# A SwiGLU first pass: every second tile summed as three 256-column products, and its head cut into pairs of channel tiles

## The chip, the core and the metric

The kernel runs on one core of a Trainium2 chip. The metric is the device time of one execution in microseconds (us). A core has a matrix engine (TensorE, "PE" in the profile; its weight loads are listed apart as "PEld"), VectorE ("DVE"), ScalarE ("ACT"), GpSimd ("POOL", unused here), and a sync engine ("SP") whose queue issues all DMA transfers of this kernel. Each engine works through its own list of instructions in the order in which the program was built.

## The reference

One layer of an encoder block on 256 tokens of 2048 channels, all in 32-bit floats: a half-step SwiGLU feed-forward, attention in two groups of heads, and a second half-step SwiGLU feed-forward. Each of the three is preceded by a norm that is shifted and scaled by vectors computed from a conditioning vector `c`, and followed by a gate of the same origin:

```python
mod = jax.nn.silu(c) @ w_ada[l] + b_ada[l]
sh1, sc1, gt1, sh2, sc2, gt2, sh3, sc3, gt3 = jnp.split(mod, N_MOD, axis=-1)
f = swiglu(modulate(rms_norm(h, g_ffn1[l]), sh1, sc1), w1_gate[l], w1_up[l], w1_down[l])
h = h + 0.5 * gt1[:, None, :] * f
# swiglu(x) = (silu(x @ w_gate) * (x @ w_up)) @ w_down ; modulate(n) = n * (1 + scale) + shift
```

The inner width is 5632. The weights (half a gigabyte with `w_ada`) are read once each.

## The kernel before

**Layout and arithmetic.** Activations are kept transposed: channels on the 128 partitions, the 256 tokens in the free dimension. So there are 16 channel tiles k and 44 inner tiles f. The matrix engine multiplies in a reduced form of 32-bit float ("fp32r"). To keep the precision each operand is split in a high part, rounded to that form, and a low part, the rest. Of the four products three count: high x high, high x low, low x high. `nx[k]` holds both parts of channel tile k of the modulated norm side by side (256 high and 256 low columns). `mm2` (L171) forms the three products with two matmuls: the weight's high part against all 512 columns (L173), and its low part against the 256 high columns (L174). The product with the activation's low part thus lands in a second half of the PSUM tile and has to be added to the first half later. `mm3` (L176, matmul on L179) does it with three matmuls of 256 columns that all sum into one half; attention uses it.

**The weights' way.** Weights come as a stream of chunks of 128 x 1024 floats, 8 blocks of 128 x 128, in the order of use. For each chunk one DMA fills one of five raw buffers (`wraw`, L157), ScalarE casts the high part "hiw" (L167) and VectorE subtracts it for the low part "low" (L168); there are four buffers of each part. `W.chunk` (L327) keeps the stream three chunks ahead of the matmuls.

**The modulation** (`w_ada`, 18432 columns of 2048) runs in the background. A step loads 128 columns of 2048 numbers (1 MB, tiles "ra" and "rx", L138, three buffers in all) and VectorE multiplies and sums them against a broadcast of silu(c) (L147). Two of them, shift and scale, let one channel tile of the norm be formed (`norm_mod`, L241: L244 on VectorE, L247 on ScalarE, L248 on VectorE; L155 prepares the scale). How many such steps go with a chunk is set by `ws.pace(rate)`: each chunk fetched adds `rate` to a credit, and each whole credit is one step. `bg_until(n)` forces steps until no more than n are left.

**The first feed-forward.** It starts while the norm isn't complete. The first 8 inner tiles take channel tiles 0 to 5 as these come (L494, plain 32-bit matmuls). Then comes the first part, the loop at L506: inner tiles 8 to 31 take channel tiles 0 to 5 (`up_first`, L355). For each tile (gate and up columns, 12 blocks, one and a half chunks) `mm2` sums into a PSUM tile "pa", ScalarE copies the first half to a tile "pt" (L359), and VectorE adds the second half (L360). In the meantime the other ten channel tiles become ready at the rate `RA`. Then `ffn` (L407) begins. Its head takes the first four inner tiles ("pb", four PSUM tiles, all there are) through the remaining channel tiles in two cuts, 6 to 11 and then 12 to 15, each cut for all four tiles; after the second a tile is finished by `up_finish` (L371: two additions of PSUM halves, tanh, products and a split). The remaining 28 of the first 32 tiles then take channel tiles 6 to 15 one after the other, the down projection of these 32 follows ("pd"), then 12 more tiles and their down projection. The second feed-forward has the same form, with 8 channel tiles in its first part and cuts at 8, 12 and 16.

**What sets the order.** The program is built as a list of instructions with dependencies, and a planner with a cost model of its own orders each engine's instructions by readiness and priority, the place in the program being the priority unless `high_priority` raises it. Here that order is planned; only attention's matmuls are placed by hand. A VectorE instruction that waits holds up everything behind it.

Of the kernel before, what the change touches and what calls it, by code (L numbers as in the profile page):

```python
# [16 lines left out]
S = 256  # L17
D = 2048
KT = D // P
# [6 lines left out]
CW = 1024  # L26
K1 = 6
K2 = 8
KM = 12
NF0 = 8  # L30
NF1 = 4
NL = 4
ND = 3
F1 = 32
# [1 line left out]
PLAN_L = ((4, 6, 9, 11), (6, 8, 11, 13), (7, 9, 12, 14), (9, 11, 14, 15))  # L36
QS = 1
PACT = 0
RA = 0.475
RB = (0.28, 0.36, 0.36, 0.3)  # L40
RQ = 0.2
RE = 0.28
RF = (0.2, 0.2, 0.1, 0.1)
# [22 lines left out]
def build(tc, a):  # L66
    nc = tc.nc
    with ExitStack() as ctx:
# [5 lines left out]
        def psum_pool(kind):  # L74

            if "cm" in pools:
                pools.pop("cm").__exit__(None, None, None)
            if kind:
                pools["cm"] = tc.tile_pool(name=f"p{kind}", bufs=4 if kind == "pair" else 8,
                                           space=bass.MemoryType.PSUM, reuse_waits="tile")  # L80
                pools["p"] = pools["cm"].__enter__()

        def pair(nm):
            return pools["p"].tile([P, 2, 512], F32, tag="b", name=nm)
# [25 lines left out]
        nx = [cp.tile([P, 2, S], F32R, tag=f"nx{k}", name=f"nx{k}") for k in range(KT)]  # L110
# [9 lines left out]
        late = []  # L120
# [50 lines left out]
        def mm2(out, lh, ll, r, first, last):  # L171

            nc.tensor.matmul(out, lh, r, start=first, stop=False)  # L173
            nc.tensor.matmul(out[:, :S], ll, r[:, 0, :], start=False, stop=last)  # L174
# [6 lines left out]
        def split(src, hi, lo):  # L181
            nc.scalar.copy(hi, src)
            nc.vector.tensor_tensor(lo, src, hi.bitcast(F32), ALU.subtract)
# [168 lines left out]

        ws = W()

        def up_first(f, part, kx):  # L355
            ps = pair("pa")
            up_mm(ps, 0, kx, True, True)
            part[f] = hp.tile([P, 2, S], F32, tag="hid", name=f"pt{f}")
            nc.scalar.copy(part[f], ps[:, :, :S])  # L359
            nc.vector.tensor_tensor(part[f], part[f], ps[:, :, S:], ALU.add)  # L360
# [5 lines left out]
        def up_mm(ps, k0, k1, first, last):  # L366
            for j in range(2):
                for k in range(k0, k1):
                    mm2(ps[:, j, :], *ws.next(), nx[k], first and k == k0, last and k == k1 - 1)

        def up_finish(f, ps, part, hid):  # L371
            if f in part:
                t = part[f]
                nc.vector.tensor_tensor(t, t, ps[:, :, :S], ALU.add)
            else:
                t = hp.tile([P, 2, S], F32, tag="hid", name="gu")
                nc.scalar.copy(t, ps[:, :, :S])
            nc.vector.tensor_tensor(t, t, ps[:, :, S:], ALU.add)
            g_, u_ = t[:, 0, :], t[:, 1, :]
            th = sp.tile([P, S], F32, tag="nt", name="th")  # L380
            nc.scalar.activation(th, g_, AF.Tanh, scale=0.5)
            nc.vector.scalar_tensor_tensor(g_, th, 1.0, g_, ALU.add, ALU.mult)
            nc.vector.scalar_tensor_tensor(g_, g_, 0.25, u_, ALU.mult, ALU.mult)
            hid[f] = hp.tile([P, 2, S], F32R, tag="hid", name=f"hd{f}")
            split(g_, hid[f][:, 0, :], hid[f][:, 1, :])

        def ffn_down(fs, hid, gate, stat=None, out=None):
            acc_ = {}
            for d, f in down_order(fs):
                if d not in acc_:  # L390
                    acc_[d] = bank("pd")
                mm2(acc_[d], *ws.next(), hid[f], f == fs[0], f == fs[-1])
                if f != fs[-1]:
                    continue
                ps = acc_[d]
                g = gate(d)
                if d == KT - 1 and stat is not None:
                    idle(9)
                with tc.high_priority(offset=URGENT if stat is not None and d >= KT - 2 else 0):
                    for part_ in (ps[:, :S], ps[:, S:]):  # L400
                        nc.vector.scalar_tensor_tensor(h[d], part_, g, h[d], ALU.mult, ALU.add)  # L401
                    if stat is not None:
                        stat.add(h[d])
                if out is not None:
                    nc.sync.dma_start(out[d], h[d])

        def ffn(kx, part, ready_k, gate, rates, stat=None, out=None):  # L407


            hid = {}  # L410
            head = [pair("pb") for f in range(NF1)]
            ready_k(KM)
            for f in range(NF1):
                up_mm(head[f], kx, KM, True, False)
            ready_k(KT)
            late[:] = [True]
            ws.pace(rates[0])
            for f in range(NF1):
                up_mm(head[f], KM, KT, False, True)
                up_finish(f, head[f], part, hid)  # L420
            for f in range(NF1, F1):
                ps = pair("pb")
                up_mm(ps, kx, KT, True, True)
                up_finish(f, ps, part, hid)
            psum_pool("bank")
            ws.pace(rates[1])
            ffn_down(range(F1), hid, gate)
            psum_pool("pair")
            ws.pace(rates[2])
            for f in range(F1, FT):  # L430
                ps = pair("pb")
                up_mm(ps, 0, KT, True, True)
                up_finish(f, ps, {}, hid)
            ln_exp_set()
            psum_pool("bank")
            ws.pace(rates[3])
            ffn_down(range(F1, FT), hid, gate, stat, out)
# [5 lines left out]
        part = {}  # L443
# [41 lines left out]
        for k in range(K1):  # L485
# [4 lines left out]
            for j in range(2):  # L490
                w = ws.whole()
                for b in range(8):
                    f, q = 4 * j + b // 2, b % 2
# [10 lines left out]

        ws.pace(RA)
        for f in range(NF0, F1):  # L506
            up_first(f, part, K1)
        st = Stat(KT)

        def rest1(k):  # L510
# [6 lines left out]
        def once(l, fn):  # L517
            def get(d):
                if (l, d) not in gates:
                    gates[l, d] = fn(d)  # L520
                return gates[l, d]
            return get
# [3 lines left out]
        def gate1(d):  # L526
            bg_until(min(len(bg) + len(pend), 4 * KT - d - 1))
            return mods[2][:, d : d + 1]

        ffn(K1, part, rest1, once(1, gate1), RB, stat=st)  # L530
        ws.pace(0.0)
        bg_until(0)
        idle(14)
# [249 lines left out]
        part = {}  # L783
# [13 lines left out]
            bg_until(min(len(bg) + len(pend), KT - d - 1))  # L797
            return mods[8][:, d : d + 1]

        ffn(K2, part, rest2, once(3, gate3), RF, out=a["out"])  # L800
        psum_pool(None)
        ax_close()

# [38 lines left out]
def _arrays(inputs):  # L842
    g = {k: np.asarray(v) for k, v in inputs.items()}
    rope, lnc, nam, idx = _consts()
    c = np.ascontiguousarray

    def vec(v):
        return np.asarray(v).reshape(-1, P).T

    arr = {  # L850
        "x": c(g["x"][0].T.reshape(4, 4, P, S).transpose(0, 2, 1, 3)),
        "w_ada": c(g["w_ada"][0].reshape(D, 9 * KT, P).transpose(1, 2, 0)),
        "vecs": c(np.concatenate([
            vec(g["g_ffn1"][0]), vec(g["g_mix"][0]), vec(g["g_ffn2"][0]),
            vec(g["g_out_na"][0]), vec(g["g_out_dil"][0]), vec(g["c"][0]), vec(g["b_ada"][0])], axis=1)),
        "qkg": c(np.stack([g["qn_na"][0], g["kn_na"][0], g["qn_dil"][0], g["kn_dil"][0]])),
        "rope": rope, "lnc": lnc, "nam": nam,
        "nab": c(g["rpb_na"][0].reshape(8, -1)[:, idx].reshape(8, 2, P, S).transpose(0, 2, 1, 3)),
        "w_qkv": c(g["w_qkv"][0].reshape(8, 2, P, 3, 4, 512).transpose(4, 3, 0, 2, 1, 5)[:, ::-1].reshape(96, P, CW)),
        "w_o": c(g["w_o"][0].reshape(2, 8, P, KT, P).transpose(0, 3, 2, 1, 4).reshape(2 * KT, P, CW)),  # L860
    }

    def stream(blocks):
        return c(blocks.reshape(-1, 8, P, P).transpose(0, 2, 1, 3).reshape(-1, P, CW))

    for l in (1, 2):
        gu = np.stack([g[f"w{l}_gate"][0], g[f"w{l}_up"][0]]).reshape(2, KT, P, FT, P)
        gu = gu.transpose(3, 0, 1, 2, 4)
        kx = K1 if l == 1 else K2
        down = g[f"w{l}_down"][0].reshape(FT, P, KT, P).transpose(2, 0, 1, 3)  # L870

        def flat(x):
            return x.reshape(-1, P, P)

        arr[f"w{l}_a"] = stream(gu[NF0 if l == 1 else 0 : F1, :, :kx])
        arr[f"w{l}_b"] = stream(np.concatenate([
            flat(gu[:NF1, :, kx:KM]), flat(gu[:NF1, :, KM:]), flat(gu[NF1:F1, :, kx:])]))
        arr[f"w{l}_c"] = stream(gu[F1:])
        for nm, fs in (("d", range(F1)), ("e", range(F1, FT))):
            d, f = np.array(list(down_order(fs))).T  # L880
            arr[f"w{l}_{nm}"] = stream(down[d, f])
        if l == 1:
            arr["w1_s"] = stream(gu[:NF0, :, :K1].transpose(2, 0, 1, 3, 4))
    return arr
# [21 lines left out]
```

## Time and profile before

| | |
|---|---|
| median of 3 runs | 1902.46 us (1902.03 to 1902.89) |
| profiled execution, its own time | 1902.98 us |
| its span, first to last instruction | 1901.2 us |
| TensorE busy | 1873.3 us (99%) |
| weight loads busy | 1633.8 us (86%) |
| VectorE busy | 1563.3 us (82%) |
| ScalarE busy | 907.4 us (48%) |
| moved by DMA | 503.98 MB, mean 265 GB/s |
| mean granted TensorE clock | 0.996 |

How to read it: the rows of the profile have a start or a count and a busy time, the engine, the line of the kernel, the operation, and the tiles written and read. "[0.60 <-ACT pt L359]" means that the engine had been idle for 0.60 us and that ScalarE's instruction on L359, which wrote tile "pt", ended that. Matmuls are pipelined and their ends modelled, so the pace of the matrix engine is read from starts and counts, not from durations. The first part starts at about 63 us and the head at about 171 us of the span.

### The profile page before, as it was taken

What the parts mean: (1) busy time and instruction counts of PE and PEld (TensorE: products, weight loads), DVE (VectorE), ACT (ScalarE), POOL (GpSimd) and SP (SyncE); (2) the same over time, 40 slices, a digit from 0 to 9 for tenths busy, and PEclk for the clock granted to TensorE, in tenths of its full rate; (3) what the DMA queues carried; (4) which work ended last, traced back from release to release, by engine and by line L of the source; (5) the groups of instructions that cost most, each with busy time, mean ns of one, the idle gap of its engine ahead of it and who ended that gap; (6) DMA issues with size and microseconds to landing.
All of it is one profiled execution on the core that took longest, in us unless ns stands there. A gap on an engine that the chain in (4) does not pass through costs nothing.

```text
span 1901.2 us, 27533 instructions
## 1 busy us (share of the span) xinstructions
PE 1873.3 (99%) x10564; PEld 1633.8 (86%) x10564; DVE 1563.3 (82%) x2123; ACT 907.4 (48%) x1333; POOL 0.7 (0%) x6
## 2 busy tenths in 40 slices
PE   8999999999999999999999999999999999999999
PEld 6877888888888888888888888888888888888888
DVE  7899999988888889878887898888799986556565
ACT  2444545443334454555555565544555543334442
POOL 0000000000000000000000000000000000000000
PEclk9999999999999999999999999999999999999999
DMA  9988888889998987777765544888677876666664
GB/s 393 397 327 299 307 301 303 303 314 337 334 328 324 334 309 247 257 260 248 263 234 174 153 154 157 320 294 303 212 276 262 279 269 220 191 194 193 191 206 135
DMA packets 120227, 503.98 MB, mean 265 GB/s; under 512 B 13344, under 2 KB 15904, under 8 KB 101664
## 3 DMA queue, kind: packets, MB, share of 16 engines
q1 hardware_dynamic: 120096, 502.24, 75.9%
q8 instruction: 82, 1.34, 0.3%
q14 instruction: 49, 0.40, 0.1%
HBM read 500.09 MB, written 2.10 MB: 264 GB/s over the span
## 4 chain that ended last, share of the span: by engine, by line
PE 89%; DVE 6%; DMA 2%; ACT 1%; issue 1%; SPq 0%; ACTq 0%; DVEq 0%
PE pb L173 23%; PE pd L173 17%; PE pb L174 11%; PE pa L173 9%; PE pd L174 8%; PE pqk L179 5%; PE pqq L179 5%; PE pa L174 4%; PE pqv L179 4%; DVE low L168 2%; DMA rx<-in_w_ada_dram 2%; PE pso L173 1%; DVE rx L147 1%; DVE ra L147 1%; PE pso L174 1%
## 5 line engine op out<-in xcount | busy, mean ns | idle before, releaser
L167 ACT CAST hiw<-rw 128x1024 fp32r<-128x1024 f32 x644 | 674.6, 1050 | 713.1 <-PE pd L173 238.5
L168 DVE TENSOR_TENSOR low<-rw,hiw 128x1024 fp32r<-128x1024 f32 x644 | 785.9, 1222 | 264.3 <-ACT hiw L167 262.9
L173 PE MATMUL pb<-nx,hiw 128*128 128x512 f32 x1920 | 654.8, 389 | 0.0
L174 PE MATMUL pb<-nx,low 128*128 128x256 f32 x1920 | 530.8, 277 | 1.2 <-DVE low L168 1.2
L173 PE MATMUL pd<-hd,hiw 128*128 128x512 f32 x1408 | 480.1, 389 | 0.0
L173 PEld LDWEIGHTS pb<-nx,hiw 128*128 128x128 f32 x1920 | 360.3, 188 | 75.7
L174 PE MATMUL pd<-hd,low 128*128 128x256 f32 x1408 | 389.1, 276 | 0.0
L174 PEld LDWEIGHTS pb<-nx,low 128*128 128x128 f32 x1920 | 360.4, 188 | 1.9 <-DVE low L168 1.8
L173 PEld LDWEIGHTS pd<-hd,hiw 128*128 128x128 f32 x1408 | 264.3, 188 | 55.5
L173 PE MATMUL pa<-nx,hiw 128*128 128x512 f32 x800 | 275.1, 391 | 1.7 <-ACT hiw L167 1.2
L174 PEld LDWEIGHTS pd<-hd,low 128*128 128x128 f32 x1408 | 264.3, 188 | 0.0
L147 DVE CUSTOM_DVE_ANT_0 ra<-ra,cb,vec 128x2048 f32<-128x2048 f32 x101 | 237.0, 2346 | 3.3 <-DMA ra<-in_w_ada_dram 3.3
L174 PE MATMUL pa<-nx,low 128*128 128x256 f32 x800 | 220.9, 278 | 4.3 <-DVE low L168 4.3
L173 PEld LDWEIGHTS pa<-nx,hiw 128*128 128x128 f32 x800 | 149.5, 188 | 34.6 <-ACT hiw L167 2.4
L174 PEld LDWEIGHTS pa<-nx,low 128*128 128x128 f32 x800 | 150.2, 188 | 7.8 <-DVE low L168 6.8
L147 DVE CUSTOM_DVE_ANT_0 rx<-rx,cb,vec 128x2048 f32<-128x2048 f32 x43 | 100.9, 2347 | 1.5 <-DMA rx<-in_w_ada_dram 1.5
L173 PE MATMUL pso<-ox,hiw 128*128 128x512 f32 x256 | 90.4, 398 | 0.0
L179 PE MATMUL pqk<-hiw,nx 128*128 128x512 f32 x256 | 84.3, 395 | 0.0
L179 PE MATMUL pqq<-hiw,nx 128*128 128x512 f32 x256 | 83.0, 393 | 0.0
L179 PE MATMUL pqv<-hiw,nx 128*128 128x512 f32 x256 | 81.4, 392 | 0.3 <-ACT nx L247 0.3
L401 DVE SCALAR_TENSOR_TENSOR h<-pd,m,h 128x256 f32<-128x256 f32 x128 | 60.8, 482 | 20.0 <-PE pd L174 17.8
L174 PE MATMUL pso<-ox,low 128*128 128x256 f32 x256 | 71.6, 280 | 0.0
(138 smaller groups left out, 1510.0 us busy)
## 6 DMA issues: line engine op xcount, KB each, us to landing
ra<-in_w_ada_dram SPq DMA_DIRECT2D x101, 1024.0 KB, 7.2
rw<-in_w_b_dram SPq DMA_DIRECT2D x144, 512.0 KB, 4.5
rw<-in_w_d_dram SPq DMA_DIRECT2D x128, 512.0 KB, 4.2
rw<-in_w_a_dram SPq DMA_DIRECT2D x100, 512.0 KB, 5.2
rw<-in_w_c_dram SPq DMA_DIRECT2D x96, 512.0 KB, 4.1
rw<-in_w_qkv_dram SPq DMA_DIRECT2D x96, 512.0 KB, 4.1
rx<-in_w_ada_dram SPq DMA_DIRECT2D x43, 1024.0 KB, 7.3
rw<-in_w_e_dram SPq DMA_DIRECT2D x48, 512.0 KB, 4.5
```

Source lines behind the costliest of these rows:

```text
L147: ins = nc.vector.tensor_tensor_reduce(out=raw, in0=raw, in1=cb, scale=1.0, scalar=vec[:, BA + i : BA + i + 1], op0=ALU.mult, op1=ALU.add, ...
L167: casts[:] = casts[-1:] + [nc.scalar.copy(hi, raw)]
L168: lows[:] = lows[-1:] + [nc.vector.tensor_tensor(lo, raw, hi.bitcast(F32), ALU.subtract)]
L173: nc.tensor.matmul(out, lh, r, start=first, stop=False)
L174: nc.tensor.matmul(out[:, :S], ll, r[:, 0, :], start=False, stop=last)
L179: nc.tensor.matmul(out, l, r, start=first and i == 0, stop=last and i == 2, **kw)
L401: nc.vector.scalar_tensor_tensor(h[d], part_, g, h[d], ALU.mult, ALU.add)
```

## The change

Three things are edited, all in the first feed-forward's way of using channel tiles.

1. `up_first` gets a flag `slim`, set for even inner tiles (8, 10, ... 30: 12 of the 24 tiles of the first part). Such a tile uses `mm3` instead of `mm2`, so its three products sum into one half of PSUM, and is stored by `park`, one copy on ScalarE; the addition L360 does not exist for it.
2. The head of `ffn` takes a list of cuts. The first feed-forward's is 6, 8, 10, 12, 14, 16 instead of 6, 12, 16; the second's stays 8, 12, 16. The chunks of `w1_b` are laid out in the new order. The rate changes from `RA` to the next one ahead of the last cut, that is after 8 chunks of the head instead of 6.
3. `RA`, the modulation steps that go with one chunk of the first part, goes from 0.475 to 0.455.

```diff
-KM = 12
+CUTS = (6, 8, 10, 12, 14, 16)
+CUTS2 = (8, 12, 16)
...
-RA = 0.475
+RA = 0.455
...
-        def up_first(f, part, kx):
+        def up_first(f, part, kx, slim=False):
             ps = pair("pa")
+            if slim:
+                for j in range(2):
+                    for k in range(kx):
+                        wh, wl = ws.next()
+                        mm3(ps[:, j, :S], wh, wl, nx[k][:, 0, :], nx[k][:, 1, :], k == 0, k == kx - 1)
+                park(ps[:, :, :S], f, part)
+                return
             up_mm(ps, 0, kx, True, True)
...
-            ready_k(KM)
-            for f in range(NF1):
-                up_mm(head[f], kx, KM, True, False)
-            ready_k(KT)
-            late[:] = [True]
-            ws.pace(rates[0])
-            for f in range(NF1):
-                up_mm(head[f], KM, KT, False, True)
-                up_finish(f, head[f], part, hid)
+            for k0, k1 in zip(cuts, cuts[1:]):
+                ready_k(k1)
+                if k1 == KT:
+                    late[:] = [True]
+                    ws.pace(rates[0])
+                for f in range(NF1):
+                    up_mm(head[f], k0, k1, k0 == kx, k1 == KT)
+                    if k1 == KT:
+                        up_finish(f, head[f], part, hid)
...
-            up_first(f, part, K1)
+            up_first(f, part, K1, f % 2 == 0)
...
-        ffn(K1, part, rest1, once(1, gate1), RB, stat=st)
+        ffn(CUTS, part, rest1, once(1, gate1), RB, stat=st)
...
-        ffn(K2, part, rest2, once(3, gate3), RF, out=a["out"])
+        ffn(CUTS2, part, rest2, once(3, gate3), RF, out=a["out"])
...
-            flat(gu[:NF1, :, kx:KM]), flat(gu[:NF1, :, KM:]), flat(gu[NF1:F1, :, kx:])]))
+            *(flat(gu[:NF1, :, k0:k1]) for k0, k1 in zip(cuts, cuts[1:])), flat(gu[NF1:F1, :, kx:])]))
```

More of the change, by code (lines that the diff above doesn't have):

```diff
@@ L405, in ffn_down, with ffn @@
                     nc.sync.dma_start(out[d], h[d])
-        def ffn(kx, part, ready_k, gate, rates, stat=None, out=None):
+        def ffn(cuts, part, ready_k, gate, rates, stat=None, out=None):
+            kx = cuts[0]
             hid = {}
             head = [pair("pb") for f in range(NF1)]
-            ready_k(KM)
-            for f in range(NF1):
-                up_mm(head[f], kx, KM, True, False)
-            ready_k(KT)
-            late[:] = [True]
-            ws.pace(rates[0])
-            for f in range(NF1):
-                up_mm(head[f], KM, KT, False, True)
-                up_finish(f, head[f], part, hid)
+            for k0, k1 in zip(cuts, cuts[1:]):
[7 more added lines that the diff above has]
+                        up_finish(f, head[f], part, hid)
             for f in range(NF1, F1):
@@ L868, in _arrays @@
         gu = gu.transpose(3, 0, 1, 2, 4)
-        kx = K1 if l == 1 else K2
+        cuts = CUTS if l == 1 else CUTS2
+        kx = cuts[0]
         down = g[f"w{l}_down"][0].reshape(FT, P, KT, P).transpose(2, 0, 1, 3)
```

## The prediction

> **What bounds the kernel now.** I read the page first, then the busy time by stretches of 50 us, then waits, idle times and the order of instructions inside the one stretch where TensorE is not full.
>
> ```profile
> span 1901.2 us, 27533 instructions
> PE 1873.3 (99%) x10564; PEld 1633.8 (86%) x10564; DVE 1563.3 (82%) x2123; ACT 907.4 (48%) x1333; POOL 0.7 (0%) x6
> ```
>
> Busy time by stretches (columns: us, then PE, weight loads, VectorE, ScalarE, GpSimd busy with their counts, clock, DMA share, GB/s):
>
> ```profile
> 50.00:100.00 50.00, 47.87 (x257) 40.87 (x256) 43.95 (x49) 23.52 (x35) 0.00 (x0) 1.00 0.97 381
> ...
> 150.00:200.00 50.00, 47.06 (x269) 40.30 (x268) 45.57 (x55) 24.53 (x32) 0.00 (x0) 1.00 0.82 297
> 200.00:250.00 50.00, 50.00 (x296) 44.20 (x295) 49.78 (x69) 25.39 (x36) 0.00 (x0) 1.00 0.85 304
> 500.00:600.00 100.00, 100.00 (x589) 88.42 (x588) 81.73 (x86) 41.37 (x44) 0.00 (x0) 1.00 0.90 329
> ```
>
> TensorE is full from 200 us on, even where VectorE is busy for 49.78 of 50. Before that it is not, and the matmul counts (257 and 269 against 296) show more loss than the busy time does. The full pace is 100.00 us / 589 matmuls = 0.1698, so 0.340 us for one block (a 512-column matmul on L173 and a 256-column one on L174). The stretch is the first part (tiles "pa") and the head of four tiles behind it ("pb"); first starts, then groups between 62 and 210 us:
>
> ```profile
> L173 PE MATMUL pa<-nx,hiw x800: 387/389/503, 63.3 to 1351.6; 128*128 128x512 f32 x160
> L173 PE MATMUL pb<-nx,hiw x1920: 387/389/403, 171.3 to 1831.4; 128*128 128x512 f32 x192
> ...
> L174 PE MATMUL pa<-nx,low 128*128 128x256 f32 x288 | 80.0, 281 | 4.3 <-DVE low L168 4.3
> ```
>
> The 288 blocks take 171.3 - 63.3 = 108.0 us; at 0.340 they would take 97.8. **10.2 us are lost.** To what, the waits between 60 and 210 us say (total us, times, longest):
>
> ```profile
> ACT pt L359 <- PE pa L174: 52.9, 22, 3.6
> PEld pa L174 <- DVE low L168: 6.8, 9, 1.1
> ...
> DVE pt L360 <- ACT pt L359: 4.2, 9, 0.6
> PEld pa L173 <- ACT hiw L167: 2.4, 4, 0.8
> PEld pb L174 <- DVE low L168: 1.8, 2, 1.0
> SPq L159 <- DVE low L168: 107.3, 49, 4.8
> ```
>
> Weight loads wait 6.8 + 2.4 = 9.2 us in the first part (the remaining 1.0 is pace, below) and 1.8 in the head: **11.0 us of stall** in all. The DMA queue itself waits 107.3 us for VectorE to free raw buffers, so data aren't what is late. The order in one stall, VectorE and then TensorE:
>
> ```profile
> 79.06 2.34 DVE L147 CUSTOM_DVE_ANT_0 ra<-ra,cb,vec 128x2048 f32<-128x2048 f32 x1
> ...
> 81.33 0.68 DVE L360 TENSOR_TENSOR pt<-pt,pa 128x512 f32<-128x512 f32 x1
> 81.93 1.22 DVE L168 TENSOR_TENSOR low<-rw,hiw 128x1024 fp32r<-128x1024 f32 x1
> 83.06 0.48 DVE L248 SCALAR_TENSOR_TENSOR nx<-nt,m,nx 128x256 fp32r<-128x256 f32 x1
> 83.46 1.22 DVE L168 TENSOR_TENSOR low<-rw,hiw 128x1024 fp32r<-128x1024 f32 x1
> 85.28 0.69 DVE L360 TENSOR_TENSOR pt<-pt,pa 128x512 f32<-128x512 f32 x1 [0.60 <-ACT pt L359]
> 85.88 2.35 DVE L147 CUSTOM_DVE_ANT_0 rx<-rx,cb,vec 128x2048 f32<-128x2048 f32 x1
> ...
> 89.29 0.68 DVE L360 TENSOR_TENSOR pt<-pt,pa 128x512 f32<-128x512 f32 x1
> 89.89 0.15 DVE L155 SCALAR_TENSOR_TENSOR m<-m,vec 128x1 f32<-128x1 f32 x1
> ```
>
> ```profile
> 88.32 0.39 PE L173 MATMUL pa<-nx,hiw 128*128 128x512 f32 x1
> 89.43 0.39 PE L174 MATMUL pa<-nx,low 128*128 128x256 f32 x1 [0.72 <-DVE low L168]
> ```
>
> Chain: TensorE ends tile 12 (an even one), ScalarE copies it, VectorE, idle since 84.6, adds the other half (L360, 85.28), then the modulation product (85.88), and only then the low part that TensorE needs at 88.3; it starts again at 89.43, 1.1 instead of 0.23 us after its last matmul. From the addition to the end of the low part it is 89.29 - 85.28 = 4.0 us, plus some 0.6 for the copy: more than the 12 x 0.340 = 4.08 us that TensorE has for a tile.
>
> **The change part by part.**
>
> *One addition in two goes.* 12 of 24 tiles lose their L360. Starts one behind the other give what an instruction occupies: addition 81.93 - 81.33 = 0.60; low part 83.06 - 81.93 = 1.13; modulation product 81.33 - 79.06 = 2.27; the norm's steps 0.40 (83.46 - 83.06) twice and 0.15 (L155) for each two products, so 2.27 + 0.48 = 2.75 a product. Work of VectorE for two tiles (three chunks), before: 3 x 1.13 + 2 x 0.60 + 3 x 0.475 x 2.75 = 3.39 + 1.20 + 3.92 = 8.51 us, against 24 x 0.3396 = 8.15 of TensorE. VectorE bounds this stage, and its waits (4.2 for the copy) come on top: 9.0 measured (108.0 / 12). After: 3.39 + 0.60 + 3 x 0.455 x 2.75 = 7.74, which is 0.41 under TensorE; over 12 pairs 4.9 us of slack. ScalarE's copy stays as it is. So TensorE bounds, except where the order still puts a wait in front. The planner orders the engines anew, which I can't see. One such order costs more than VectorE's sum, the copy ahead of a cast:
>
> ```profile
> 93.63 0.59 ACT L359 COPY pt<-pa 128x512 f32<-128x512 f32 x1 [3.58 <-PE pa L174]
> 94.12 1.05 ACT L167 CAST hiw<-rw 128x1024 fp32r<-128x1024 f32 x1
> ...
> 95.22 0.50 PE L173 MATMUL pa<-nx,hiw 128*128 128x512 f32 x1 [0.26 <-ACT hiw L167]
> 96.48 0.39 PE L174 MATMUL pa<-nx,low 128*128 128x256 f32 x1 [0.76 <-DVE low L168]
> ```
>
> ScalarE idles 3.58 us until tile 14 (even) ends mid-chunk, and casts the next chunk only then; TensorE loses 0.26 + 0.76 idle and some 0.5 of refilling, 1.5 us (95.22 to 96.48 is 1.26 instead of 0.23 alone). The waits above hold four for a cast, 2.4 us in all, so some three of this size. The copy stays in the change, and 0 to 3 x 1.5 = 4.5 us may stay with it; I take one, 1.5, because the slack lets casts run ahead.
>
> *Three 256-column products instead of 512 + 256.* The columns are the same (768), with one matmul and one weight load more in each of 12 x 12 = 144 blocks. The kernel has such triples in attention; chain of waits, then matmuls by time, the first and the last of six:
>
> ```profile
> 870.39 0.70 PE po L179 x6
> ```
>
> ```profile
> 1118.16 0.28 PE L179 MATMUL po<-ph,vh 128*128 128x256 f32 x1
> ...
> 1118.73 0.28 PE L179 MATMUL po<-ph,vl 128*128 128x256 f32 x1
> ```
>
> That is 0.70 / 6 = 0.117 in the one place and 0.57 / 5 = 0.114 in the other: 0.342 to 0.351 for a triple against 0.340, so 144 x 0.002 to 0.011 = 0.3 to 1.6 us more. No run of triples longer than two is in this trace, so I let the cost go down to 0 and take 1.0. (The Trainium skill, page "TensorE: Matmul & The Clock Gate", section "Back-to-back issue gap", speaks against the change: in a stream of load-and-multiply pairs a 128-column matmul takes about 81 ns where an isolated one takes 56. If each matmul more cost those 25 ns, an estimate from that page is 144 x 0.025 = 3.6 us and a time near 1897; the rows above, with 114 to 117 ns for half of 227, show 1 to 4.) The same slower pace is in ordinary blocks too and explains the 1.0 us of the loss that isn't stall; I leave it as it is.
>
> *RA 0.475 to 0.455, and the head in five cuts.* 37 chunk loads fall to the pass and 6 to the head: 37 x 0.475 gives 17 modulation steps and 43 x 0.475 gives 20. Then 37 x 0.455 gives 16 and 45 x 0.455 gives 20. One product (2.75 us of VectorE) and its 1 MB transfer move from the pass to the head, past some chunk loads in SP's one queue, which has the time (it waits 107 us). The last channel tile is due after 64 blocks of the head rather than 48, 16 x 0.340 = 5.4 us later, which covers the 2.75; without that cover it would stand on TensorE's path in full. In the head the two waits (1.8 us) follow the last even tile and go with the rest. New is that the four head tiles end 4 x 0.340 = 1.36 us apart, not 2.72. Tile 4 needs the first one's PSUM, drained by two additions of L360's form (1.20), 4.1 us after that one ends; with a modulation product and a low part queued in front it takes 1.20 + 2.27 + 1.13 = 4.6, so 0 to 0.5 us; I take 0.3. The steps from there to the first down projection are the same (80 chunks less 6 or 8, and 74 x 0.28 and 72 x 0.28 both give 20), chunks are as many, and TensorE is full behind, so what is won here reaches the end.
>
> **Sum.** 11.0 - 1.5 (cast) - 1.0 (triples) - 0.3 (head) = 8.2 us. The profiled execution took 1902.98 (span 1901.2 and 1.8 around it), 0.5 above the median of 1902.46; from the median, 1902.5 - 8.2 = **1894.3 us**. With nothing left it is 11.0 + 0.5 of pace: 1891.0.
>
> **The rivals.**
>
> *The copy goes on holding back the cast* (0.17). Waits on ScalarE and triples at their worst: 11.0 - 4.5 - 1.6 - 0.5 = 4.4, 1898.1. For it: the copy is not removed and ScalarE idles 52.9 us for it. Against it: the waits above came where VectorE was behind.
>
> *DMA becomes the bound* (0.10). Sizes, and two stretches of 10 us:
>
> ```profile
> rw<-in_w_a_dram SPq DMA_DIRECT2D x100, 512.0 KB, 5.2
> ra<-in_w_ada_dram SPq DMA_DIRECT2D x101, 1024.0 KB, 7.2
> ```
>
> ```profile
> 70.00:80.00 10.00, 10.00 (x59) 8.79 (x58) 9.52 (x11) 3.73 (x5) 0.00 (x0) 1.00 1.00 403
> 130.00:140.00 10.00, 10.00 (x59) 8.75 (x58) 9.87 (x12) 4.50 (x6) 0.00 (x0) 1.00 0.98 358
> ```
>
> Two tiles at full pace need 3 x 0.524 + 1.365 x 1.049 = 3.00 MB in 8.15 us, 368 GB/s. If 358 is all there is, a pair takes 8.38, 12 x 0.23 = 2.8 us more: 1897.1. Against it stand 403 GB/s and the queue's idle time. (The Trainium skill, page "DMA: Bandwidth & Descriptors", section "Where 436 GB/s comes from", puts the limit of loads from memory at about 358 GB/s a core; the second row agrees, the first does not.)
>
> *The stalls stay* (0.11): the new order puts something else ahead of the low parts, and VectorE idles in the freed time: 0 to 2 us won, 1901.5. Against it: VectorE's sum falls below TensorE's.
>
> *Weight loads set the pace of the triples: slower* (0.04). A load takes 188 ns:
>
> ```profile
> L174 PEld LDWEIGHTS pb<-nx,low 128*128 128x128 f32 x1920 | 360.4, 188 | 1.9 <-DVE low L168 1.8
> ```
>
> Were three of them in a row not to overlap in a long run, a triple would take 0.564 and the 144 blocks 144 x 0.224 = 32 us more: 1902.5 - 9.2 + 32 = 1925 (9.2 is the sum without its 1.0 for triples). It decides from 0.340 + 9.2 / 144 = 0.40 us a triple on. Against it: six in 0.70.
>
> **How the numbers follow.** The forecast has 0.58. A change of 0.2% (3.8 us, below 1898.7 or above 1906.3) is about what can be told from none. Faster: 0.56 of the forecast, half of the cast's 0.17, DMA's 0.10, 0.01 of the stalls that stay: 0.76. Slower: the weight loads' 0.04 and 0.02 of the stalls that stay (a worse order). Same: the other 0.18. The range goes from all stalls gone, 1891.0, less 0.5 for the unknown pace, to 1900.0, which takes in the cast and DMA and leaves out most of the last two rivals.
>
> **What would show it.** Right: L360 12 instead of 24 times in the first part; "pa" to "pb" (63.3 to 171.3) down to some 101 us; weight loads' waits for low parts and casts in that stretch from 11 to about 2; triples at 0.34 to 0.35. The cast rival shows as ScalarE casts behind an idle copy with TensorE waiting for "hiw"; DMA as VectorE or ScalarE waiting for "ra" or "rw"; the weight loads as a pace over 0.36 with no wait. Wrong: fewer than 4 us won in the first part, or a loss of the same size behind 200 us.

## The result and the profile after

The changed kernel takes 1895.58 us (median of 6 runs, 1895.43 to 1896.07) against 1902.5 us (6 runs of the kernel before beside it): 6.9 us less, a ratio of 0.9965 with a 95% interval of 0.9952 to 0.9978. The forecast was 1894.3, 8.2 us less. It is faster by more than the 0.2% that can be told apart. Times here and below are of fast runs; one run of e5 (5124 us) and one of e8 (2078 us) were far slower and are left out.

The page, and busy time by stretches of the changed kernel (columns as before: us, then PE, weight loads, VectorE, ScalarE, GpSimd busy with counts, clock, DMA share, GB/s):

```profile
span 1893.7 us, 27811 instructions
PE 1870.2 (99%) x10708; PEld 1639.9 (87%) x10708; DVE 1555.3 (82%) x2111; ACT 907.6 (48%) x1333; POOL 0.7 (0%) x6
```

```profile
50.00:100.00 50.00, 49.38 (x322) 45.08 (x322) 43.74 (x48) 25.55 (x37) 0.00 (x0) 1.00 0.99 388
150.00:200.00 50.00, 48.91 (x302) 43.50 (x301) 44.33 (x56) 26.13 (x34) 0.00 (x0) 1.00 0.79 288
200.00:250.00 50.00, 50.00 (x296) 44.23 (x295) 50.00 (x68) 24.57 (x34) 0.00 (x0) 1.00 0.86 315
500.00:600.00 100.00, 100.00 (x589) 88.48 (x589) 83.14 (x87) 41.55 (x46) 0.00 (x0) 1.00 0.91 329
```

TensorE has 144 matmuls more (10708 - 10564) and VectorE 12 instructions fewer (2123 - 2111), as the change says. Behind 200 us nothing moved: 296 and 589 matmuls in the same stretches. The gain lies between 63 us and the first down projection. First and last starts: the down projection ("pd") before and after, then the first part and the head after (line numbers are now 1 to 8 higher; L180 is the triple, L174 and L175 are the pair of matmuls, L368 the addition, L148 the modulation product, L169 the low part):

```profile
L173 PE MATMUL pd<-hd,hiw x1408: 389/389/394, 391.4 to 1896.9; 128*128 128x512 f32 x176
L174 PE MATMUL pd<-hd,hiw x1408: 389/389/394, 384.2 to 1889.3; 128*128 128x512 f32 x176
...
L180 PE MATMUL pa<-nx,hiw x288: 276/280/385, 63.0 to 160.4; 128*128 128x256 f32 x144
L174 PE MATMUL pb<-nx,hiw x1920: 388/389/398, 166.1 to 1823.9; 128*128 128x512 f32 x192
```

The first part takes 166.1 - 63.0 = 103.1 us instead of 108.0, and from there to the first down projection it is 384.2 - 166.1 = 218.1 instead of 391.4 - 171.3 = 220.1. What is left of the waits between 60 and 210 us:

```profile
ACT pt L372 <- PE pa L180: 24.8, 12, 2.9
ACT pt L367 <- PE pa L175: 24.2, 12, 3.3
...
DVE pt L368 <- ACT pt L367: 4.9, 6, 1.2
PEld pa L175 <- DVE low L169: 1.9, 2, 1.4
DVE pt L382 <- PE pb L175: 1.9, 1, 1.9
...
ACT hiw L168 <- DMA rw<-in_w_b_dram: 1.4, 1, 1.4
PEld pa L180 <- DVE low L169: 0.6, 3, 0.2
```

Weight loads wait 1.9 + 0.6 = 2.5 us for low parts, none for casts and none in the head; before it was 11.0. The stall that was shown of before (tile 12) reads so now, VectorE:

```profile
83.10 1.22 DVE L169 TENSOR_TENSOR low<-rw,hiw 128x1024 fp32r<-128x1024 f32 x1
84.23 2.34 DVE L148 CUSTOM_DVE_ANT_0 rx<-rx,cb,vec 128x2048 f32<-128x2048 f32 x1
86.50 0.08 DVE L148 DVE_READ_ACCUMULATOR2_ANT m<- 128x1 f32 x1
86.62 0.16 DVE L156 SCALAR_TENSOR_TENSOR m<-m,vec 128x1 f32<-128x1 f32 x1
86.81 0.49 DVE L245 SCALAR_TENSOR_TENSOR nt<-h,m,rsr 128x256 f32<-128x256 f32 x1
87.22 1.22 DVE L169 TENSOR_TENSOR low<-rw,hiw 128x1024 fp32r<-128x1024 f32 x1
```

The product follows the low part at once (84.23); there is no wait for a copy and no addition between them, and the next low part starts at 87.22 instead of 88.15. The one large stall left is of another make, an odd tile's addition with a product and the norm behind it, VectorE and then TensorE:

```profile
157.06 0.69 DVE L368 TENSOR_TENSOR pt<-pt,pa 128x512 f32<-128x512 f32 x1 [0.89 <-ACT pt L367]
...
158.06 1.22 DVE L169 TENSOR_TENSOR low<-rw,hiw 128x1024 fp32r<-128x1024 f32 x1
159.19 2.35 DVE L148 CUSTOM_DVE_ANT_0 rx<-rx,cb,vec 128x2048 f32<-128x2048 f32 x1
...
162.18 3.49 DVE L169 TENSOR_TENSOR low<-rw,hiw 128x1024 fp32r<-128x1024 f32 x3
```

```profile
161.97 0.39 PE L174 MATMUL pa<-nx,hiw 128*128 128x512 f32 x1
163.45 0.38 PE L175 MATMUL pa<-nx,low 128*128 128x256 f32 x1 [1.09 <-DVE low L169]
```

### The profile page after: what moved, and what is told of

It reads as the page before. It is cut to its first block, busy times and chain, and to the rows that moved or that the text cites. A ratio compares the mean times of both kernels' runs of the same rounds, so it can differ in the third digit from the quotient of the medians.

```text
span 1893.7 us, 27811 instructions
## 1 busy us (share of the span) xinstructions
PE 1870.2 (99%) x10708; PEld 1639.9 (87%) x10708; DVE 1555.3 (82%) x2111; ACT 907.6 (48%) x1333; POOL 0.7 (0%) x6
## 4 chain that ended last, share of the span: by engine, by line
PE 91%; DVE 5%; DMA 2%; ACT 1%; issue 1%; SPq 0%; ACTq 0%; DVEq 0%
PE pb L174 23%; PE pd L174 17%; PE pb L175 12%; PE pd L175 8%; PE pa L174 8%; PE pqk L180 5%; PE pqq L180 5%; PE pqv L180 4%; PE pa L175 4%; PE pa L180 2%; DVE low L169 2%; DMA rx<-in_w_ada_dram 2%; PE pso L174 1%; DVE rx L148 1%; PE pso L175 1%
## 5 line engine op out<-in xcount | busy, mean ns | idle before, releaser
L169 DVE TENSOR_TENSOR low<-rw,hiw 128x1024 fp32r<-128x1024 f32 x644 | 785.0, 1222 | 261.9 <-ACT hiw L168 260.6
L174 PE MATMUL pb<-nx,hiw 128*128 128x512 f32 x1920 | 654.5, 389 | 0.0
L175 PE MATMUL pb<-nx,low 128*128 128x256 f32 x1920 | 530.3, 276 | 0.0
L174 PE MATMUL pd<-hd,hiw 128*128 128x512 f32 x1408 | 480.1, 389 | 0.0
L174 PEld LDWEIGHTS pb<-nx,hiw 128*128 128x128 f32 x1920 | 360.3, 188 | 75.5
L175 PE MATMUL pd<-hd,low 128*128 128x256 f32 x1408 | 389.1, 276 | 0.0
L175 PEld LDWEIGHTS pb<-nx,low 128*128 128x128 f32 x1920 | 360.4, 188 | 0.2
L174 PEld LDWEIGHTS pd<-hd,hiw 128*128 128x128 f32 x1408 | 264.3, 188 | 55.4
L175 PEld LDWEIGHTS pd<-hd,low 128*128 128x128 f32 x1408 | 264.3, 188 | 0.0
L148 DVE CUSTOM_DVE_ANT_0 ra<-ra,cb,vec 128x2048 f32<-128x2048 f32 x101 | 236.9, 2346 | 3.3 <-DMA ra<-in_w_ada_dram 3.3
L174 PE MATMUL pa<-nx,hiw 128*128 128x512 f32 x656 | 224.9, 390 | 0.6 <-DVE nx L249 0.4
L175 PE MATMUL pa<-nx,low 128*128 128x256 f32 x656 | 180.9, 277 | 1.3 <-DVE low L169 1.3
L174 PEld LDWEIGHTS pa<-nx,hiw 128*128 128x128 f32 x656 | 122.9, 188 | 26.4 <-DVE nx L249 1.5
L175 PEld LDWEIGHTS pa<-nx,low 128*128 128x128 f32 x656 | 123.1, 188 | 2.3 <-DVE low L169 1.9
L148 DVE CUSTOM_DVE_ANT_0 rx<-rx,cb,vec 128x2048 f32<-128x2048 f32 x43 | 100.9, 2346 | 1.5 <-DMA rx<-in_w_ada_dram 1.5
L174 PE MATMUL pso<-ox,hiw 128*128 128x512 f32 x256 | 90.0, 397 | 0.0
L180 PE MATMUL pqk<-hiw,nx 128*128 128x512 f32 x256 | 84.4, 395 | 0.0
L180 PE MATMUL pqq<-hiw,nx 128*128 128x512 f32 x256 | 83.0, 393 | 0.0
L180 PE MATMUL pqv<-hiw,nx 128*128 128x512 f32 x256 | 81.5, 392 | 0.3 <-ACT nx L248 0.3
L175 PE MATMUL pso<-ox,low 128*128 128x256 f32 x256 | 71.4, 279 | 0.0
```

Of the source, the lines that this page charges most:

```text
L148: ins = nc.vector.tensor_tensor_reduce(out=raw, in0=raw, in1=cb, scale=1.0, scalar=vec[:, BA + i : BA + i + 1], op0=ALU.mult, op1=ALU.add, ...
L169: lows[:] = lows[-1:] + [nc.vector.tensor_tensor(lo, raw, hi.bitcast(F32), ALU.subtract)]
L180: nc.tensor.matmul(out, l, r, start=first and i == 0, stop=last and i == 2, **kw)
```

## The experiments

Twelve kernels, each compared with the kernel before on the same chip (1902.0 to 1902.4 there). Each edit is shown against the changed kernel. e3 and e8, which price a triple, stand further below and not in the table. "Waits" is the sum of the weight loads' waits for low parts and casts between 60 and 210 us in its profiled execution, as above.

| kernel | triples | RA | cuts | median us | ratio to before, 95% | waits us |
|---|---|---|---|---|---|---|
| before | none | 0.475 | 2 | 1902.5 | | 11.0 |
| change | even | 0.455 | 5 | 1895.58 | 0.9965 (0.9952 to 0.9978) | 2.5 |
| e1 | none | 0.455 | 5 | 1899.77 | 0.9985 (0.9977 to 0.9994) | 8.6 |
| e2 | even | 0.475 | 2 | 1897.86 | 0.9975 (0.9965 to 0.9986) | 4.4 |
| e4 | odd | 0.455 | 5 | 1898.37 | 0.9981 (0.9972 to 0.9990) | 5.6 |
| e5 | none | 0.455 | 2 | 1899.65 | 0.9984 (0.9975 to 0.9993) | 8.4 |
| e6 | none | 0.475 | 5 | 1901.88 | 0.9997 (0.9988 to 1.0005) | 11.3 |
| e7 | every 4th | 0.455 | 5 | 1897.29 | 0.9974 (0.9965 to 0.9984) | 5.3 |
| e9 | even | 0.455 | 2 | 1895.98 | 0.9970 (0.9959 to 0.9980) | 2.5 |
| e10 | even | 0.475 | 5 | 1897.41 | 0.9978 (0.9969 to 0.9987) | 4.2 |
| e11 | all 24 | 0.455 | 5 | 1896.24 | 0.9971 (0.9962 to 0.9981) | 1.4 |
| e12 | even | 0.435 | 5 | 1894.82 | 0.9964 (0.9951 to 0.9976) | 0.4 |

**e1, the change without its triples.**

```diff
-            up_first(f, part, K1, f % 2 == 0)
+            up_first(f, part, K1, False)
```

> RA 0.455 and the five cuts, but no tile summed as three products. My theory (VectorE's addition for the even tiles is what makes the low parts late): VectorE's work for two tiles is 3.39 + 1.20 + 3.75 = 8.34 us against TensorE's 8.15, so it still bounds the first part; that part stays near 106 to 108 us (108.0 before, 103.1 after the change), only the head's 1.8 us go, and the time is 1899 to 1902. Rival (the modulation spread out and the later due times are what helped): the first part falls to about 100 to 103 us and the time is 1893 to 1897, since the triples' cost is saved too.

2.5 us less than before, within what my theory gave for the time. By first starts the first part went to 103.9 us (63.5 to 167.4), which lies between the two ranges. That measure misleads here: the new order has one matmul of the head, with its wait for a cast, ahead of the last 15 matmuls of the first part:

```profile
167.36 0.50 PE L174 MATMUL pb<-nx,hiw 128*128 128x512 f32 x1 [0.44 <-ACT hiw L168]
...
170.17 0.28 PE L175 MATMUL pa<-nx,low 128*128 128x256 f32 x1
170.30 0.28 PE L175 MATMUL pb<-nx,low 128*128 128x256 f32 x1
```

The first part ends at 170.3, which is 106.8 us after its start, some 1.0 of them the head's matmul and its wait. That is near the 106 to 108 of my theory and not the 100 to 103 of the rival. The weight loads' waits in e1:

```profile
PEld pa L175 <- DVE low L169: 6.7, 10, 1.1
...
PEld pb L174 <- ACT hiw L168: 0.8, 1, 0.8
```

The waits for low parts stay at 6.7 us as before (6.8). So the triples are what takes these.

**e2, the triples alone.**

```diff
-RA = 0.455
+RA = 0.475
-CUTS = (6, 8, 10, 12, 14, 16)
+CUTS = (6, 12, 16)
```

> Even tiles as three products, RA 0.475 and two cuts as before. My theory: VectorE's work for two tiles is 3.39 + 0.60 + 3.92 = 7.91 us, under TensorE's 8.15, so nearly the whole gain of the change is here: first part 103 to 104 us, time 1896 to 1898. Rival (spread modulation helped): first part 107 to 108 and the triples' price on top, 1902 to 1905.

4.4 us less than before and a first part of 103.6 us: the theory's ranges, the rival's excluded. Some two thirds of the gain are the triples'; the 4.4 and e1's 2.5 add to the 6.9 of the change, each of these with an interval of some 2 us to either side.

**e4, odd tiles instead of even ones.**

```diff
-            up_first(f, part, K1, f % 2 == 0)
+            up_first(f, part, K1, f % 2 == 1)
```

> The changed kernel with the odd tiles (which end at a chunk's end) summed as three products instead of the even ones (which end in the middle of a chunk). VectorE's sum is the same. If that sum alone decides: first part about 103 us, 1895 to 1896.5. If the place of the addition decides (before, VectorE's waits for a copy stood almost all at even tiles): additions of even tiles stay ahead of modulation product and low part, stalls of about 1 us stay at some of them, first part 105 to 107 and 1897.5 to 1900.

3.9 us less instead of 6.9, with the same work on each engine. VectorE and TensorE at the place of tile 12:

```profile
85.51 0.69 DVE L368 TENSOR_TENSOR pt<-pt,pa 128x512 f32<-128x512 f32 x1 [0.62 <-ACT pt L367]
86.12 2.34 DVE L148 CUSTOM_DVE_ANT_0 rx<-rx,cb,vec 128x2048 f32<-128x2048 f32 x1
...
89.11 2.59 DVE L169 TENSOR_TENSOR low<-rw,hiw 128x1024 fp32r<-128x1024 f32 x2
```

```profile
88.71 0.39 PE L174 MATMUL pa<-nx,hiw 128*128 128x512 f32 x1
90.38 0.39 PE L175 MATMUL pa<-nx,low 128*128 128x256 f32 x1 [1.28 <-DVE low L169]
```

The chain of the kernel before is back: wait for the even tile's copy, addition, product (here with a step of the norm too), and only then the low part. The first part, counted to its end at 170.4 as in e1, takes 107.0 us. The sum of VectorE's work is not enough to tell; it matters which addition goes. The odd tiles' additions are not worth nothing: against e1 the waits fall by 3.0 us here, by 6.1 with the even ones (the change).

**e7, every fourth tile.**

```diff
-            up_first(f, part, K1, f % 2 == 0)
+            up_first(f, part, K1, f % 4 == 0)
```

> The changed kernel with every fourth tile (8, 12, ... 28) as three products instead of every second. VectorE's work for two tiles is 3.39 + 0.90 + 3.75 = 8.04 us, 0.1 under TensorE's 8.15; half of the additions in mid-chunk stay in front of products and low parts. If the place of each addition decides: stalls of some 4 us in place of 1.6 and 0.9 us less for triples, 1897 to 1898.5. If VectorE's sum decides, it is still under: 1894.5 to 1895.5.

1897.29, in the range that goes with the place of each addition: 5.2 us less than before instead of 6.9, and the rate's share is in both.

**e5 and e6, the rate alone and the cuts alone** (both without triples; e5 with the two old cuts, e6 with the old rate).

```diff
-            up_first(f, part, K1, f % 2 == 0)
+            up_first(f, part, K1, False)
-CUTS = (6, 8, 10, 12, 14, 16)     # e5
+CUTS = (6, 12, 16)                # e5
-RA = 0.455                        # e6
+RA = 0.475                        # e6
```

> Only RA 0.455, two cuts and no triples. RA and cuts together took the stalls of the first part and the head from 9.0 us to 6.5 and the time to 1899.8. My theory: the lower rate does it in the first part (VectorE's work for two tiles 8.51 to 8.34 us, 2.0 us over 12 pairs): 1899.5 to 1901. Rival (the cuts, by letting the planner put products later, do it): no difference, 1901.5 to 1903.

> Only the five cuts, RA 0.475 and no triples. My theory: the cuts touch the head alone, whose two waits are 1.5 us: 1901 to 1902.5. Rival: they carry what RA and cuts gave together, 1899.5 to 1900.5.

The rate gives all that the two gave together (2.8 us; together 2.5). The cuts give 0.6 us at the medians with an interval across 1: nothing that can be told from none.

**e9 and e10, the change without its cuts, and without its rate.**

```diff
-CUTS = (6, 8, 10, 12, 14, 16)     # e9
+CUTS = (6, 12, 16)                # e9
-RA = 0.455                        # e10
+RA = 0.475                        # e10
```

> The changed kernel with the head in two cuts as before (triples for even tiles, RA 0.455). If cuts add nothing beside the other two: 1895 to 1896.5. If they are what keeps the head free of stalls once the first part is faster (the last channel tiles come due 5.4 us earlier without them): one or two waits of 0.7 to 1.3 us near the head, 1896.5 to 1898.5.

> The changed kernel with RA 0.475 (triples for even tiles, five cuts). RA alone took 2.8 us, triples alone 4.4. If both work on the same loss (VectorE's work for two tiles is 7.91 us here, already under TensorE's): 1896 to 1897.5. If they add up: 1897.5 to 1899.

Without the cuts the time is that of the change within the runs' spread, with the same waits: beside the other two they bring nothing here, and the head has no wait without them either. Without the rate two waits of 1.5 us in all are back in the head, and the time is 1.4 us above e9's on the same chip (1.8 above the change's), with intervals that overlap. By the waits, rate and triples overlap a little: they take 2.6 (e5) and 6.6 us (e2) alone and 8.5 together (e9). The times, 2.8 and 4.4 alone and 6.0 together, agree with that but are too rough to show it.

**e3, what a triple costs.** All 32 tiles of the second feed-forward's first part, where TensorE never waits, as triples on top of the change.

```diff
-            up_first(f, part, K2)
+            up_first(f, part, K2, True)
```

> The changed kernel, and all 32 tiles of the second feed-forward's first part summed as three products too (384 blocks). That part showed no wait of TensorE worth naming, so this measures the price of a triple by itself. If what I read in the changed kernel's slim tiles holds (52.95 us for 144 blocks, 0.36 to 0.368 a triple against 0.340): 384 x 0.021 to 0.028 = 8 to 11 us more than the changed kernel, 1903.5 to 1906.5. If the attention's six in 0.70 holds (0.342 to 0.351): 1 to 4 us more, 1896.5 to 1900. If weight loads don't overlap in long runs (0.564): 86 us more.

1902.02 us, ratio to before 0.9996 (0.9987 to 1.0006): some 6.4 us more than the change. I had miscounted: the part has 32 x 16 = 512 blocks, not 384. The stretch from 1200 to 1340 us lies wholly in it; the changed kernel's row, then e3's:

```profile
1200.00:1340.00 140.00, 140.00 (x824) 123.84 (x823) 112.38 (x124) 69.75 (x85) 0.00 (x0) 1.00 0.84 290
```

```profile
1200.00:1340.00 140.00, 140.00 (x1191) 140.00 (x1190) 97.09 (x99) 67.74 (x82) 0.00 (x0) 1.00 0.82 284
```

A pair takes 140.00 / (824 / 2) = 0.3398 us, a triple 140.00 / (1191 / 3) = 0.3526, 0.0128 more; 512 of these are 6.6 us, which is the time lost. In the first part of the changed kernel eight triples in a row (156.24 to 159.06 us) take 0.3525 each, the same. And the weight loads are busy for 140.00 of 140 instead of 123.84.

**e8, what sets that price.** The third product of each triple of e3 is left out for half of the tokens (128 columns instead of 256), in the second feed-forward's first part alone, so the output lacks that share. The edit against e3, without the flag that selects it:

```diff
-  mm3(ps[:, j, :S], wh, wl, nx[k][:, 0, :], nx[k][:, 1, :], k == 0, k == kx - 1)
+  nc.tensor.matmul(ps[:, j, :S], wh, nx[k][:, 0, :], start=k == 0, stop=False)
+  nc.tensor.matmul(ps[:, j, :S], wh, nx[k][:, 1, :], start=False, stop=False)
+  nc.tensor.matmul(ps[:, j, :P], wl, nx[k][:, 0, :P], start=False, stop=k == kx - 1)
```

> All 32 tiles of the second feed-forward's first part as triples (these are 512 blocks, not the 384 that I counted for the run with full triples, whose 6.7 us more are thus 0.013 us a triple, 0.353), and the third product of each left out for half of the tokens: the low part of these weights against 128 columns instead of 256, so the output lacks that share. If the weight loads set the pace of a triple (0.118 for each load, whatever is streamed): 0.353 a triple as with full ones, time 1901 to 1903. If the columns set it: 640 of 768 columns, 0.29 to 0.30, 512 x 0.055 = 28 us less, 1872 to 1875.

1898.71 us, ratio to before 0.9983 (0.9973 to 0.9994), 3.3 less than e3: between the two ranges, close to the first. The same stretch in e8:

```profile
1200.00:1340.00 140.00, 140.00 (x1213) 140.00 (x1212) 97.77 (x97) 68.76 (x83) 0.00 (x0) 1.00 0.82 287
```

A sixth of the columns less saves 0.3526 - 140.00 / (1213 / 3) = 0.0064 us a triple, where columns alone would save 0.0566 (a sixth of 0.3398); 512 x 0.0064 is the 3.3 us. So the columns don't set the pace of a triple, and neither does a fixed cost of 0.0128 a matmul on top of the columns, which would save nearly as much. What is left is a least time of 0.115 to 0.118 for each matmul with its load. That it is the load's fits the loads being busy for all of the time, but no run here parts it from another least time of a matmul.

**e11, all tiles as triples.**

```diff
-            up_first(f, part, K1, f % 2 == 0)
+            up_first(f, part, K1, True)
```

> The changed kernel with all 24 tiles of the first part as triples, no addition on VectorE. Stalls of 1.6 us can go at most, and the triples' price doubles, 144 x 0.013 = 1.9 us more: 1895.5 to 1898 if weight loads set it; below 1894.5 if triples cost nothing in this stretch.

1896.24 us, in the range for a price set by the loads and 0.7 more than the change, which the intervals don't part: waits go from 2.5 to 1.4 us, and the additional 144 triples cost 144 x 0.0128 = 1.8.

**e12, a still lower rate.**

```diff
-RA = 0.455
+RA = 0.435
```

> The changed kernel with RA 0.435: one modulation product less in the first part (15.9 steps over 37 chunks give 16 still, 45 x 0.435 gives 19, so one is forced ahead of the last cut). If VectorE's remaining load is what leaves 1.6 us of stall: 1894 to 1895.5, faster than the changed kernel. If the forced product is late in the head: 1896 to 1898.

(37 x 0.435 is 16.1 and gives 16 steps; only their places among the chunks change in the first part.) 1894.82 us, in the range for VectorE's remaining load, and in the trace almost nothing of the stalls is left:

```profile
PEld pa L180 <- ACT pt L372: 0.2, 1, 0.2
PEld pa L180 <- DVE low L169: 0.2, 1, 0.2
PEld pa L175 <- DVE low L169: 0.2, 1, 0.2
```

It is faster than the kernel before. Against the changed kernel it is 0.8 us at the medians and 0.9964 against 0.9965 in ratio, which doesn't part them; the trace says that it has less to wait for, but it is that of the shortest of the five runs (1893.67).

## Why the prediction was right, and where it was off

**What bounds, and the chain.** Right, and shown: with triples alone the waits fall from 11.0 to 4.4 us and the time by 4.4 (e2); with the same number of triples at the odd tiles the chain stands where it stood (e4). The sum of VectorE's work (8.51 to 7.74 us for two tiles) pointed the right way but would have given e4 and e7 the full gain. It takes the chain as well to explain the runs. The first part came to 103.1 us where I had expected some 101: 97.8 at full pace, 1.0 of slower pace as before, 1.8 for triples and 2.5 of waits.

**Stalls left.** I had taken 1.5 us in the first part and 0.3 in the head; 2.5 and 0 were left, 8.5 us recovered instead of 9.2. The make was wrong: no weight load waits for a cast any more, so the rival of the copy ahead of the cast did not come. What was left is waits for low parts, for which the sum had nothing; the largest, 1.4 us, stands behind a product and a norm (163.45 us above). That the 1.5 kept for the cast covered most of it is luck. The head's crowding at its end, 0 to 0.5, cost nothing: VectorE even waits there for TensorE (L382, 1.9 us).

**Triples.** This is the term that was mis-sized: 1.0 us, with 0.3 to 1.6 as its bounds from the attention's rows, against 144 x 0.0128 = 1.8. The nearest row was the upper one, 0.70 us for six (0.351 a triple; 0.353 measured in a long run). I went below it on account of attention's last triples at 0.114 a pass, which are but six matmuls behind pairs; a long row goes at the upper pace. The rival of loads that don't overlap at all (0.564) is excluded by e3, but its direction was right: with triples the loads are busy for all of the time, and a triple takes a little more than its columns. The Trainium skill, page "TensorE: Matmul & The Clock Gate", section "LDWEIGHTS (loading the stationary operand)", gives a load of 128 columns as 128 / 1.2 ns, by estimate 107 ns; the runs show 115 to 118 ns for a load with its matmul in a stream, and 113 ns for each 256 columns in a pair with a longer pass. The 25 ns a matmul that I drew from the same page's rule on streams, 3.6 us, is twice what was measured.

With both terms as measured, 8.5 - 1.8 = 6.7 us, against 6.9 in the runs.

**Rate and cuts.** I priced them as one product moved and covered, with no term of their own in the sum. The rate was worth 2.8 us alone and 1.4 to 1.8 on top of the triples; my own ledger held it (3.92 to 3.75 us for two tiles, 2.0 over 12 pairs). The cover that the cuts were to give was not needed (e9).

**DMA.** The rival did not come. The casts waited for weight chunks for 1.4 us in the head (the row above) and 0.3 us at another place, and TensorE did not wait for that. The stretch from 50 to 100 us moved 388 GB/s, and the first part as a whole (63 to 166 us) 362, more than the 358 of that rival. The DMA engines were busy for 0.96 of that time, so there was little room.

## What to carry to other kernels

When an engine is nearly as busy as the one it feeds, its sum of work is not enough to go by; look in its order for an instruction that waits for the fed engine and stands ahead of what that engine needs next, and take away that instruction there first (the even tiles' additions took 6.1 us of waits, as many at the odd tiles 3.0). Splitting a matmul into shorter ones to save an addition costs weight loads: check how busy these are first; here they were busy for 88% of the time, and one load more in each block made that all of it and cost 0.013 us a block. And of several edits made together, time each alone: one of the three here brought nothing that could be told.

## What the runs showed of the hardware

A stream of 256-column matmuls, each with its own weight load of 128 x 128, runs at 0.1175 us a matmul with the weight loads busy for all of the time (e3), and cutting a third of these matmuls to 128 columns brings that to 0.1154 only (e8). In the pair of 512 and 256 columns the loads have time to spare (123.84 of 140 us, the changed kernel), and 768 columns take 0.3398 us, 0.1133 for each 256. The granted clock was 1.00 in all three stretches.
